# Gate tiles of a hybrid mixer read ahead, two heads' attention steps called later, one warming product fewer

## The chip, the cores and the metric

The kernel runs on one core of one Trainium2 chip, as one launch. The metric is device time in microseconds (us): lower is better. A run is one execution; the median of the runs shown is the time that is compared. One further execution was taken with the hardware profiler; all durations of single instructions come from it.

## The reference, cut to what matters

One block on x of 512 rows by 1024 columns, float32: half a SwiGLU feed-forward step, a mixer, half a SwiGLU step, a norm.

```
x = x + 0.5 * swiglu(rmsnorm(x), ffn1)              # 1024 -> 2 * 2816 -> 1024
h = rmsnorm(x)
cb, cc, cu, q, k, v, g_lr, r, ga, gb = split(h @ w_in)
y_conv = (cb * short_conv(cc * cu)) @ w_out_conv
o      = gla_chunked(q, k, v, log_sigmoid(g_lr @ up + b) / 16)   # 4 heads, chunks of 64
y_gla  = (norm(o) * silu(r)) @ w_out_gla
x = x + (sigmoid(ga) * y_conv + sigmoid(gb) * y_gla) @ w_o
x = x + 0.5 * swiglu(rmsnorm(x), ffn2)
return rmsnorm(x)
```

ga and gb are 512 x 1024 each. The kernel holds each as eight tiles of 128 x 512 (four blocks of rows t, two halves of columns e).

## The kernel before

**Products.** Every operand v is split into a high part h (a cast to the short fp32r type, on ACT) and a low part l = v - h (a subtraction, on DVE), and a product is three products: h·h, h·l, l·h. For weights this is `W.issue`: L380 makes wh on ACT, L381 makes wl on DVE. The tiles wh and wl have three buffers each, and W runs two steps ahead of PE. So each step of PE (12 products of 512 columns at L696, or 24 of 256 columns at L613) needs one L380 and one L381 of its own before its second product.

**Strassen-like steps.** Large products go in seven steps (m1, p2, q6, p5, q7, p3, p4) over quarter matrices. The weights' quarters a11, a12, a21, a22 are loaded by SP (L343, 512 KB each) into tiles f. Sums of quarters are made in three ways: by POOL as accumulating DMAs (L347: a21 += a22, then after m1 a11 += a21, then after p2 a12 += a11), by DVE for q7 (L374: a11 -= a22, which must wait until the accumulating DMA of a12 += a11 has read a11), and by DVE at L359 for the sets. A "tall" product (names v, ga, gb, out) runs each step twice, for two halves s = 0 and 1 of the inner dimension; a "set" (numbered 0 to 7) runs it once.

**Order of the work.** The mixer runs: q and k; the talls v, ga, gb; the eight sets (four for the convolution, two for cb, two for r); the tall out (y_conv); w_out_gla in two halves e; w_o. Inside `run_sets` PE's order is the program's, by a manual schedule. DVE, ACT, SP and POOL are ordered by a scheduler, which sees the order of the calls and its own estimate of when operands are ready; `keep_in_program_order` only keeps an instruction behind the one called before it on its engine.

**Hooks.** Between steps, the table `hooks` calls the pieces of the attention of each head: `gates` (decays' logarithms), `decays` (two DVE subtractions, L1336 and L1339), `exps` (five small activations on ACT), `scale`, `scale_k`, `scale_q` (nine DVE multiplications through `mul`, L583), `scores` (PE products L1385, L1387, transposes L1398), `state` (PE L1410, DVE L1414), `output` (PE L1427, L1430), `squares`, `normalise`. A key such as ("gb", 0, "p2") means: after half 0 of step p2 of gb; (3, "m1") means: after step m1 of set 3.

**Gates.** When a tile of ga or gb is complete, ACT stores it to DRAM (L1484). While w_out_gla runs, `gate` (L1684) takes a free working tile tp, reads the tile back on SP's queue (L1686, 256 KB), applies the sigmoid on ACT (L1687) and DVE multiplies: m = y_conv * sigmoid(ga) at L583, then, when a half of w_out_gla is done, the product with sigmoid(gb) (L583) and the sum (L1726). PE needs m only for the transposes L1699 ahead of w_o.

**Start.** Ten products of ones (L277, each two passes on PE) fill PE's time until the first operands are there.

Of the kernel before, what the change touches and what calls it, by code (L numbers as in the profile page):

```python
# [11 lines left out]
AF = mybir.ActivationFunctionType  # L12
# [15 lines left out]
NTB = S // P  # L28
# [6 lines left out]

V_G1, V_GM, V_G2, V_GLA, V_CONV, V_GB = 0, 8, 16, 24, 32, 56
NVEC = 60
WARM = 10
ODD_FILL = 272

TAIL = 4
# [191 lines left out]
def block_kernel(ctx: ExitStack, tc: tile.TileContext, xT, vecs, gf, gup, wgl, wts, out):  # L233
    nc = tc.nc
# [20 lines left out]
    def tile_of(pool, shape, dtype=F32):  # L255
        cnt[0] += 1
        return pools[pool].tile(shape, dtype, tag=pool, name=f"{pool}{cnt[0]}")

    def T(dtype=F32):
        return tile_of("tp", [P, S], dtype)  # L260
# [5 lines left out]
    def AUX():  # L266
        cnt[0] += 1
        return pa.tile([P, S], F32, tag="aux", name=f"aux{cnt[0]}")
# [6 lines left out]
    warm = AUX()  # L275
    for i in range(WARM):
        nc.tensor.matmul(warm[:, :P], ones, ones, start=True, stop=True)  # L277
# [6 lines left out]
    def big(name):  # L284
        return keep.tile([P, KD, S], F32, tag="X", name=name)
# [296 lines left out]
    def mul(out_, a, b, eng=None):  # L582
        (eng or nc.vector).tensor_tensor(out=out_, in0=a, in1=b, op=ALU.mult)  # L583
# [608 lines left out]
    def mixer(norm, nxt):  # L1192
# [3 lines left out]
        gates_d = {n: dram.tile([KD, P, S], F32, tag=n, name=n) for n in ("ga", "gb")}  # L1196
# [7 lines left out]
        def flat(i):  # L1204
            at = 2 * (S + 2) * i
            return YS.rearrange("p e t -> p (e t)")[:, at : at + 1024]

        def two(i):
            return flat(i).rearrange("p (e t) -> p e t", e=2)
# [6 lines left out]
        def G_tile(i, dtype=F32):  # L1216
            cnt[0] += 1
            return pools["g"].tile([P, S], dtype, tag=f"g{i}", name=f"g{i}_{cnt[0]}")

        sc = pools["g"].tile([P, S], F32, tag="sc", name="sc")  # L1220
# [9 lines left out]
            out=maskf, in_=maskf, pattern=[[1, P]], compare_op=ALU.is_ge, fill=0.0,  # L1230
# [76 lines left out]
        def pairs(t):  # L1307
            return t.rearrange("p (b e t) -> p b e t", e=2, t=CH)
# [10 lines left out]
        def gates(h):  # L1319

            a = AUX()
            nc.tensor.matmul(a, gup_w[:R3, h * DK : (h + 1) * DK], glr[:R3],
                             start=True, stop=True)
            b = vec[:, V_GB + h : V_GB + h + 1]
            nc.scalar.activation(E, a, AF.Abs, bias=b)
            nc.vector.tensor_scalar(out=M, in0=a, scalar1=b, scalar2=0.0,
                                    op0=ALU.add, op1=ALU.min)
            nc.scalar.activation(E, E, AF.Exp, scale=-1.0)
            nc.scalar.activation(E, E, AF.Ln, bias=1.0)
            nc.vector.tensor_tensor(out=M, in0=M, in1=E, op=ALU.subtract)  # L1330
            nc.vector.tensor_tensor_scan(out=E, data0=reset, data1=M, initial=0.0,
                                         op0=ALU.mult, op1=ALU.add)
# [18 lines left out]
        def bc(t):  # L1351
            return t.unsqueeze(2).to_broadcast([P, NTB, CH])

        def scale(h):

            q_, k_ = QK[h][:, 0], QK[h][:, 1]
            ref = sm4[:, 0]
            mul(q_, EX, q_)  # L1360
            mul(KX, pairs(KS)[:, :, 0], pairs(k_)[:, :, 0])
            mul(QX, pairs(q_)[:, :, 1], bc(ref[:, :, 1]))

        def scale_k(h):

            k_, dc = QK[h][:, 1], sm4[:, 1]
            mul(pairs(KS)[:, :, 1], pairs(KS)[:, :, 1], pairs(k_)[:, :, 1])
            mul(k_, M, k_)
            mul(pairs(KS)[:, :, 0], KX, bc(dc[:, :, 1]))

        def scale_q(h):

            q_ = QK[h][:, 0]
            ref, dc = sm4[:, 0], sm4[:, 1]
            mul(pairs(QS)[:, :, 1], QX, bc(dc[:, :, 0]))
            mul(pairs(QS)[:, :, 0], pairs(q_)[:, :, 0], bc(ref[:, :, 0]))
            mul(d2s, dc[:, :, 0], dc[:, :, 1])

        def scores(h):

            q_, k_ = QK[h][:, 0], QK[h][:, 1]
            st = AUX()
            for t in range(NTB):
                b = slice(t * P, (t + 1) * P)
                nc.tensor.matmul(st[:, b], k_[:, b], q_[:, b], start=True, stop=True)  # L1385
            for t in range(NTB):
                nc.tensor.matmul(st[:CH, t * P + CH : (t + 1) * P], KX[:, t], QX[:, t],  # L1387
                                 start=True, stop=True)
            nc.vector.copy_predicated(
                sc.rearrange("p (b i) -> p b i", i=P),  # L1390
                mask.unsqueeze(1).to_broadcast([P, NTB, P]),
                st.rearrange("p (b i) -> p b i", i=P),
            )
            n = NTB - 1
            tr = AUX()
            for t in range(n):
                b = slice(t * P, (t + 1) * P)
                nc.tensor.transpose(tr[:, b], KS[:, b], ident)  # L1398
            nc.scalar.copy(E[:, : n * P], tr[:, : n * P])

        def state(h):

            v = vt[h // 2]
            kvs = []
            for t in range(NTB - 1):
                if t % 2 == 0:
                    kv = AUX()
                hc = slice((t % 2) * DV, (t % 2) * DV + DV)
                kvs.append(kv[:, hc])
                nc.tensor.matmul(kvs[t], E[:, t * P : (t + 1) * P],  # L1410
                                 v[t][:, (h % 2) * DV : (h % 2) * DV + DV], start=True, stop=True)
            nc.scalar.copy(ST[0], kvs[0])
            for t in range(1, NTB - 1):
                nc.vector.scalar_tensor_tensor(out=ST[t], in0=ST[t - 1], scalar=d2s[:, t : t + 1],  # L1414
                                               in1=kvs[t], op0=ALU.mult, op1=ALU.add)
# [114 lines left out]
        def split_o(h):  # L1530
            for a, b in split_pair(O[h]):
                og_h.append(a)
                og_l.append(b)

        hooks = {
            ("v", 0, "q6"): [decays, exps], ("v", 1, "p5"): [lambda: scale(0)],
            ("v", 0, "q7"): [lambda: scale_k(0)],
# [1 line left out]
            ("ga", 1, "m1"): [lambda: state(0)], ("ga", 1, "p2"): [lambda: output(0)],  # L1539
            ("ga", 0, "p5"): [lambda: squares(0)], ("ga", 1, "p5"): [lambda: gates(1)],  # L1540
            ("ga", 0, "q7"): [decays], ("ga", 1, "q7"): [exps],
            ("ga", 0, "p3"): [lambda: scale(1)], ("ga", 1, "p3"): [lambda: scale_k(1)],
            ("gb", 0, "m1"): [lambda: scores(1)], ("gb", 1, "m1"): [lambda: scale_q(1)], ("gb", 0, "p2"): [lambda: state(1)],
            ("gb", 1, "q6"): [lambda: output(1)], ("gb", 1, "q7"): [lambda: squares(1)],
            ("gb", 0, "p3"): [move], ("gb", 1, "p3"): [lambda: gates(2)],
            ("gb", 0, "p4"): [decays], (0, "p2"): [exps], (0, "q6"): [lambda: scale(2)],
            (0, "p5"): [lambda: scale_k(2)], (0, "q7"): [lambda: scale_q(2)],
            (0, "p3"): [lambda: scores(2)], (1, "q6"): [lambda: state(2)],
            (1, "q7"): [lambda: output(2)], (1, "p4"): [lambda: squares(2)],
            (1, "p3"): [lambda: gates(3)], (2, "p5"): [decays], (2, "q7"): [exps],  # L1550
            (3, "m1"): [lambda: scale(3)], (2, "p4"): [lambda: scale_k(3)],
            (2, "p3"): [lambda: scale_q(3)],
            (3, "q6"): [lambda: scores(3)], (3, "p3"): [lambda: state(3)],
            (4, "q6"): [lambda: output(3)], (4, "p3"): [lambda: squares(3)],
            (5, "q7"): [lambda: normalise(0)], (5, "p3"): [lambda: normalise(1)],
            (6, "q7"): [lambda: normalise(2)], (6, "p3"): [lambda: normalise(3)],
            ("out", 1, "p5"): [lambda: co.make("p4")], ("out", 0, "q7"): [lambda: split_o(0)],
            ("out", 1, "q7"): [lambda: split_o(1)], ("out", 0, "p3"): [lambda: split_o(2)],
            ("out", 1, "p3"): [lambda: split_o(3)],
        }  # L1560
# [116 lines left out]
        m = [[QK[2 + t // 2][:, t % 2] for t in range(NTB)], vt[1]]  # L1677
        co = Operands(lambda j, l: YS[:, 4 * j : 4 * j + 4, 2 + l * HW : 2 + (l + 1) * HW])
# [3 lines left out]
        finish_late()  # L1682

        def gate(name, t, e):  # L1684
            g = T()
            tc.keep_in_program_order(nc.sync.dma_start(g, gates_d[name][2 * t + e]))  # L1686
            nc.scalar.activation(g, g, AF.Sigmoid)  # L1687
            return g

        m_h, m_l = [], []  # L1690
# [16 lines left out]
        def between(e):  # L1707
            def extra(k):
                if e == 1 and k == 3:
                    XS.append(big("X2"))  # L1710
                    x[:] = [XS[-1][:, k] for k in range(KD)]
                    for k_ in range(KD):
                        nc.gpsimd.dma_start(x[k_], xs[k_])
                if k in (1, 3, 4, 6):
                    t = (1, 3, 4, 6).index(k)
                    mul(m[e][t], m[e][t], gate("ga", t, e))
                if e == 1 and k in (5, 6):
                    turned(2 * (k - 5))
            return extra

        for e in range(2):
            o = mm_wide("w_out_gla", KD, 512 * e, og_h, og_l, extra=between(e))
            for t in range(NTB):
                g = gate("gb", t, e)
                mul(g, o[t], g)
                nc.vector.tensor_tensor(out=m[e][t], in0=m[e][t], in1=g, op=ALU.add)  # L1726

# [83 lines left out]
```

## Time and profile before

| | us |
|---|---|
| median of 3 runs | 1168.81 (1168.37 to 1169.87) |
| the profiled execution's own time | 1169.12 |
| its span, first to last instruction | 1167.4 |
| PE busy | 1158.9 |
| DVE busy | 895.1 |
| ACT busy | 657.3 |
| granted TensorE clock | 0.999 of full speed |

The profiled execution's time is 1.7 us over its span, and 0.3 us over the median. In the page's rows a group of instructions is named by line, engine and operation and by its tiles, out<-in. Rows of the timeline give the start (us from the span's start), the duration, the engine, the line and the tiles; a count such as x2 merges instructions that follow each other, and a bracket tells how long the engine was idle before and what ended that. Products of PE overlap: two that follow each other without a wait start 0.227 us (512 columns) or 0.12 us (256 columns) apart, though each is shown as longer.

### The profile page before, as it was taken

How to read it: one execution, taken by the hardware profiler on the slowest of the kernel's cores; microseconds unless marked ns; L12 is line 12 of the kernel's file. 1: busy time of each engine (PE TensorE's matmuls, PEld its weight loads, DVE VectorE, ACT ScalarE, POOL GpSimd, SP SyncE). 2: the span in 40 equal slices, each digit the busy share in tenths (PEclk: the TensorE clock that was granted, in tenths of full speed). 3: DMA queues.
4: the chain of work that ended last, by engine and by line, in shares of the span. 5: the costliest groups of instructions: out<-in, count | busy, mean ns of one | idle time of the engine just before them, and what ended most of it. 6: DMA issues, size and time to landing. Idle time of an engine off the chain costs nothing.

```text
span 1167.4 us, 16527 instructions
## 1 busy us (share of the span) xinstructions
PE 1158.9 (99%) x6428; PEld 1010.3 (87%) x6428; DVE 895.1 (77%) x1066; ACT 657.3 (56%) x832; POOL 127.4 (11%) x167
## 2 busy tenths in 40 slices
PE   9999999999999999999999999999999999999997
PEld 7888888989988888889999998888888888888886
DVE  7985666889887976777797999555876666799966
ACT  6565555634452756475654577525655556575543
POOL 0101110001120110110110112000101101101100
PEclk9999999999999999999999999999999999999999
DMA  9667786657665485878576787834567966877711
GB/s 363 129 183 165 170 219 162 173 131 175 170 207 153 96 223 152 209 208 215 134 174 155 181 205 213 288 109 131 118 181 163 231 171 157 203 176 165 184 48 72
DMA packets 59870, 203.22 MB, mean 174 GB/s; under 512 B 6960, under 2 KB 7088, under 8 KB 59792
## 3 DMA queue, kind: packets, MB, share of 16 engines
q0 software_dynamic: 20288, 73.41, 33.3%
q1 hardware_dynamic: 36912, 124.27, 32.4%
q10 hardware_dynamic: 2592, 4.49, 1.0%
q8 instruction: 50, 0.82, 0.3%
q14 instruction: 28, 0.23, 0.1%
HBM read 124.55 MB, written 8.39 MB: 114 GB/s over the span
## 4 chain that ended last, share of the span: by engine, by line
PE 95%; DVE 2%; ACT 1%; DMA 1%; issue 0%; SPq 0%; ACTq 0%; DVEq 0%
PE mm L696 48%; PE mm L613 23%; PE mm L432 5%; PE mm L408 3%; PE mm L410 3%; PE mm L409 3%; PE aux L840 1%; PE mm L451 1%; PE mm L450 1%; PE mm L449 1%; PE mm L1083 1%; PE mm L1082 1%; PE mm L1081 1%; PE aux L1427 1%; DVE wl L381 1%
## 5 line engine op out<-in xcount | busy, mean ns | idle before, releaser
L380 ACT CAST wh<-f 128x1024 fp32r<-128x1024 f32 (+1 forms) x349 | 365.5, 1049 | 361.3 <-PE mm L696 138.0
L381 DVE TENSOR_TENSOR wl<-f,wh 128x1024 fp32r<-128x1024 f32 (+1 forms) x349 | 424.1, 1217 | 181.2 <-ACT wh L380 180.4
L696 PE MATMUL mm<-wh,op 128*128 128x512 f32 x1680 | 528.1, 391 | 0.0
L696 PEld LDWEIGHTS mm<-wh,op 128*128 128x128 f32 x1680 | 315.5, 188 | 65.8 <-ACT tp L814 0.8
L696 PE MATMUL mm<-wl,op 128*128 128x512 f32 x840 | 327.3, 390 | 0.2 <-DVE wl L381 0.2
L613 PE MATMUL mm<-op,wh 128*128 128x256 f32 x1456 | 263.7, 284 | 0.2 <-ACT tp L618 0.2
L613 PEld LDWEIGHTS mm<-op,wh 128*128 128x128 f32 x1456 | 227.0, 191 | 1.1 <-ACT tp L618 0.4
L347 POOL DMA_DIRECT2D f<-f x132 | 113.8, 865 | 910.5 <-DVE wl L381 434.1
L613 PE MATMUL mm<-op,wl 128*128 128x256 f32 x728 | 206.1, 283 | 0.3 <-DVE wl L381 0.3
L696 PEld LDWEIGHTS mm<-wl,op 128*128 128x128 f32 x840 | 157.8, 188 | 32.6 <-DVE wl L381 1.0
L613 PEld LDWEIGHTS mm<-op,wl 128*128 128x128 f32 x728 | 139.1, 191 | 0.5 <-DVE wl L381 0.5
L668 ACT CAST op<-hid 128x1024 fp32r<-128x1024 f32 x42 | 44.0, 1050 | 23.2 <-PE mm L696 11.0
L669 DVE TENSOR_TENSOR op<-hid,op 128x1024 fp32r<-128x1024 f32 x42 | 51.1, 1217 | 2.9 <-ACT op L668 2.9
L408 PE MATMUL mm<-op,wh 128*128 128x512 f32 x132 | 51.4, 389 | 0.0
L409 PE MATMUL mm<-op,wh 128*128 128x512 f32 x132 | 51.4, 389 | 0.0
L410 PE MATMUL mm<-op,wl 128*128 128x512 f32 x132 | 51.4, 389 | 0.0
L432 PE MATMUL mm<-op,wh 128*128 128x512 f32 x192 | 48.3, 393 | 0.3 <-ACT wh L380 0.2
L374 DVE TENSOR_TENSOR f<-f,f 128x1024 f32<-128x1024 f32 x30 | 36.6, 1220 | 10.9 <-DMA f<-f 8.6
L432 PEld LDWEIGHTS mm<-op,wh 128*128 128x128 f32 x192 | 35.6, 188 | 8.8 <-ACT wh L380 1.1
L408 PEld LDWEIGHTS mm<-op,wh 128*128 128x128 f32 x132 | 24.8, 188 | 5.2
L409 PEld LDWEIGHTS mm<-op,wh 128*128 128x128 f32 x132 | 24.8, 188 | 5.2
L410 PEld LDWEIGHTS mm<-op,wl 128*128 128x128 f32 x132 | 24.8, 188 | 5.1
(326 smaller groups left out, 1194.8 us busy)
## 6 DMA issues: line engine op xcount, KB each, us to landing
f<-wts SPq DMA_DIRECT2D x219, 512.0 KB, 4.3
f<-f POOLq DMA_DIRECT2D x132, 512.0 KB, 5.1
X<-xT SPq DMA_DIRECT2D x8, 256.0 KB, 5.7
xs<-X POOLq DMA_DIRECT2D x8, 256.0 KB, 2.8
ga<-tp ACTq DMA_DIRECT2D x8, 256.0 KB, 5.2
gb<-tp ACTq DMA_DIRECT2D x8, 256.0 KB, 3.9
tp<-ga SPq DMA_DIRECT2D x8, 256.0 KB, 5.1
X<-xs POOLq DMA_DIRECT2D x8, 256.0 KB, 7.3
```

What stands on the lines that cost most here:

```text
L347: nc.gpsimd.dma_start(out_, a, accum_op=ALU.add)
L374: nc.vector.tensor_tensor(out=a11, in0=a11, in1=a22, op=ALU.subtract)
L380: nc.scalar.copy(h[:, :w], raw[:, :w])
L381: nc.vector.tensor_tensor(out=l[:, :w], in0=raw[:, :w], in1=h[:, :w].bitcast(F32), op=ALU.subtract)
L408: nc.tensor.matmul(o, wh, ah, start=first, stop=False)
L409: nc.tensor.matmul(o, wh, al, start=False, stop=False)
L410: nc.tensor.matmul(o, wl, ah, start=False, stop=last)
L432: nc.tensor.matmul(o[c], w[:, s : s + P], a[k], start=k == 0 and j == 0, stop=k == kt - 1 and j == 2)
L613: nc.tensor.matmul(to, ww[:, s], aa[:, t], start=fresh and k == 0 and e == 0 and j == 0, stop=k == 3 and j == 2, skip_group_check=True)
L668: nc.scalar.copy(hv, v)
L669: nc.vector.tensor_tensor(out=lv, in0=v, in1=hv.bitcast(F32), op=ALU.subtract)
L696: nc.tensor.matmul(self.bank[b][e], aa[:, c], ww, start=fresh and i == 0 and n == 0, stop=k == 3 and n == 2, skip_group_check=True)
```

## The change

It does four things.

1. **All sixteen gate tiles are read ahead, into tiles that are free by then.** The four tiles (ga, e = 0) go into three tiles of the attention (G_tile 2, 3 and 4) and `sc`; the hook `fetch_gates` after ("out", 0, "m1") issues their reads. The four (gb, e = 0) go into the lower half of the convolution's tile YS, called after ("out", 0, "q7"); the four (ga, e = 1) into its upper half, after ("out", 0, "p4"); the four (gb, e = 1) into the first four tiles again, at k = 0 of the second half of w_out_gla. Working tiles tp are no longer taken for gates.
2. **Sigmoids stand at fixed places**: of (ga, e = 0) in hooks of the tall out, the others at k = 1, 3, 4, 6 of the two halves of w_out_gla. Their number is the same, sixteen, and so are the reads.
3. **Steps of heads 1 and 3 are called later.** Head 1: scale, scale_k, scores, scale_q and state, by one or two half steps. Head 3: decays, exps, scale and scale_k, by one step.
4. **WARM is 9, not 10.**

```
-WARM = 10
+WARM = 9
...
+        ahead = {}
+
+        def fetch_gates():
+            for t, g in enumerate((G_tile(2), G_tile(3), G_tile(4), sc)):
+                tc.keep_in_program_order(nc.sync.dma_start(g, gates_d["ga"][2 * t]))
+                ahead[t] = g
+
+        def open_gate(t):
+            tc.keep_in_program_order(nc.scalar.activation(ahead[t], ahead[t], AF.Sigmoid))
+
+        def fetch_more(name, e):
+            for t in range(NTB):
+                g = two(2 * e + t // 2)[:, t % 2]
+                tc.keep_in_program_order(nc.sync.dma_start(g, gates_d[name][2 * t + e]))
+                ahead[name, t, e] = g
...
-            ("ga", 0, "p3"): [lambda: scale(1)], ("ga", 1, "p3"): [lambda: scale_k(1)],
-            ("gb", 0, "m1"): [lambda: scores(1)], ("gb", 1, "m1"): [lambda: scale_q(1)], ("gb", 0, "p2"): [lambda: state(1)],
+            ("ga", 1, "p3"): [lambda: scale(1)], ("ga", 1, "p4"): [lambda: scale_k(1)],
+            ("gb", 1, "m1"): [lambda: scores(1)], ("gb", 0, "p2"): [lambda: scale_q(1)],
+            ("gb", 1, "p2"): [lambda: state(1)],
...
-            (1, "p3"): [lambda: gates(3)], (2, "p5"): [decays], (2, "q7"): [exps],
-            (3, "m1"): [lambda: scale(3)], (2, "p4"): [lambda: scale_k(3)],
+            (1, "p3"): [lambda: gates(3)], (2, "q7"): [decays], (3, "m1"): [exps],
+            (2, "p4"): [lambda: scale(3)], (3, "p2"): [lambda: scale_k(3)],
...
+            ("out", 0, "m1"): [fetch_gates], ("out", 1, "q6"): [lambda: open_gate(0)],
+            ("out", 0, "p5"): [lambda: open_gate(1)],
+            ("out", 1, "p5"): [lambda: co.make("p4"), lambda: open_gate(2)],
+            ("out", 0, "q7"): [lambda: split_o(0), lambda: fetch_more("gb", 0)],
+            ("out", 0, "p4"): [lambda: fetch_more("ga", 1), lambda: open_gate(3)],
...
-            g = T()
-            tc.keep_in_program_order(nc.sync.dma_start(g, gates_d[name][2 * t + e]))
-            nc.scalar.activation(g, g, AF.Sigmoid)
+            g = ahead[name, t, e]
+            tc.keep_in_program_order(nc.scalar.activation(g, g, AF.Sigmoid))
...
+                if e == 1 and k == 0:
+                    for t in range(NTB):
+                        ahead["gb", t, 1] = ahead[t]
+                        tc.keep_in_program_order(
+                            nc.sync.dma_start(ahead[t], gates_d["gb"][2 * t + 1]))
...
-                    mul(m[e][t], m[e][t], gate("ga", t, e))
+                    mul(m[e][t], m[e][t], ahead[t] if e == 0 else gate("ga", t, e))
+                    gate("gb", t, e)
...
-                g = gate("gb", t, e)
+                g = ahead["gb", t, e]
```

**Where instructions move.** First DVE's queue around head 1's scaling, in the steps p3 and p4 of the tall ga (L381 is a step's wl, L583 with y or g the scaling of head 1, L1469 a sum of the tall ga). Before:

```order
L583 TENSOR_TENSOR g_538_3455<-g_538_3455,y_3223 128x4x64
L583 TENSOR_TENSOR g_539_3456<-g_538_3455,y_3223 128x256
L583 TENSOR_TENSOR g_539_3456<-y_3223,sm 128x256
L381 TENSOR_TENSOR wl_4221<-f_3851,wh_4220 128x1024
L1469 SCALAR_TENSOR_TENSOR tp_4082<-mm_4086,tp_4082 128x512
L1469 SCALAR_TENSOR_TENSOR tp_4084<-mm_4087,tp_4084 128x512
L583 TENSOR_TENSOR y_3223<-g_537_3454,y_3223 128x512
L583 TENSOR_TENSOR g_538_3455<-g_539_3456,sm 128x4x64
L381 TENSOR_TENSOR wl_4244<-f_4143,wh_4243 128x1024
```

The same place now:

```order
L583 TENSOR_TENSOR g_538_3454<-g_538_3454,y_3222 128x4x64
L381 TENSOR_TENSOR wl_4217<-f_3850,wh_4216 128x1024
L1469 SCALAR_TENSOR_TENSOR tp_4081<-mm_4085,tp_4081 128x512
L1469 SCALAR_TENSOR_TENSOR tp_4083<-mm_4086,tp_4083 128x512
L583 TENSOR_TENSOR g_539_3455<-g_538_3454,y_3222 128x256
L583 TENSOR_TENSOR g_539_3455<-y_3222,sm 128x256
L381 TENSOR_TENSOR wl_4240<-f_4142,wh_4239 128x1024
L583 TENSOR_TENSOR y_3222<-g_537_3453,y_3222 128x512
```

Two small multiplications moved behind the first L381 and the two L1469, and a full and a small one behind the second L381. Further on, in gb, the two L1414 of head 1's state moved behind the two L1469 and a L381, and on PE the scores and the state of head 1 stand 12 products later.

Second, DVE's queue around head 3's decays (L1579 and L1581 are the convolution; after the change these two lines are L1600 and L1602). Before:

```order
L1581 SCALAR_TENSOR_TENSOR y_3223<-y_3223,vec,tp_5304 128x512
L1581 SCALAR_TENSOR_TENSOR y_3223<-y_3223,vec,tp_5308 128x512
L1336 TENSOR_TENSOR g_537_3454<-g_536_3453 128x512
L1339 TENSOR_TENSOR g_538_3455<-g_536_3453 128x512
L381 TENSOR_TENSOR wl_5323<-f_4786,wh_5322 128x1024
```

Now:

```order
L1602 SCALAR_TENSOR_TENSOR y_3222<-y_3222,vec,tp_5303 128x512
L1602 SCALAR_TENSOR_TENSOR y_3222<-y_3222,vec,tp_5307 128x512
L381 TENSOR_TENSOR wl_5320<-f_4785,wh_5319 128x1024
L1336 TENSOR_TENSOR g_537_3453<-g_536_3452 128x512
L1339 TENSOR_TENSOR g_538_3454<-g_536_3452 128x512
```

The step's wl moved ahead of both subtractions.

Third, DVE's queue in the tall out, around q7's weights (L374 with its two halves, the L381 of p5's two halves, L1674, now L1695, a split of the attention's result). Before:

```order
L374 TENSOR_TENSOR f_6452<-f_6452,f_6458 128x1024
L381 TENSOR_TENSOR wl_6756<-f_6456,wh_6755 128x1024
L374 TENSOR_TENSOR f_6521<-f_6521,f_6527 128x1024
L381 TENSOR_TENSOR wl_6772<-f_6525,wh_6771 128x1024
L669 TENSOR_TENSOR op_6838<-y_3223,op_6837 128x1024
L1674 TENSOR_TENSOR op_6860<-O,op_6859 128x1024
L381 TENSOR_TENSOR wl_6798<-f_6452,wh_6797 128x1024
```

Now:

```order
L374 TENSOR_TENSOR f_6451<-f_6451,f_6457 128x1024
L374 TENSOR_TENSOR f_6520<-f_6520,f_6526 128x1024
L381 TENSOR_TENSOR wl_6762<-f_6455,wh_6761 128x1024
L381 TENSOR_TENSOR wl_6778<-f_6524,wh_6777 128x1024
L669 TENSOR_TENSOR op_6846<-y_3222,op_6845 128x1024
L1695 TENSOR_TENSOR op_6869<-O,op_6868 128x1024
L583 TENSOR_TENSOR qk_3223<-qk_3223,g_995_6688 128x512
L381 TENSOR_TENSOR wl_6805<-f_6451,wh_6804 128x1024
```

Both L374 now stand ahead of the L381 of p5's first half, and a gate's multiplication stands ahead of the L381 of q7's first half. On ACT the table load and one sigmoid stand ahead of the L380 of p5's first half, and on SP the four reads of (ga, e = 0) stand ahead of the last two weight loads that were issued before 700 us, and the four of (gb, e = 0) right behind those. POOL's order is unchanged.

More of the change, by code (lines that the diff above doesn't have):

```diff
@@ L1556, in mixer @@
             (6, "q7"): [lambda: normalise(2)], (6, "p3"): [lambda: normalise(3)],
-            ("out", 1, "p5"): [lambda: co.make("p4")], ("out", 0, "q7"): [lambda: split_o(0)],
+            ("out", 0, "m1"): [fetch_gates], ("out", 1, "q6"): [lambda: open_gate(0)],
[3 more added lines that the diff above has]
+            ("out", 0, "p4"): [lambda: fetch_more("ga", 1), lambda: open_gate(3)],
             ("out", 1, "q7"): [lambda: split_o(1)], ("out", 0, "p3"): [lambda: split_o(2)],
```

## Prediction

> **What bounds the kernel now.** I read the page's table of engines first, then PE's waits, then the timeline wherever PE waited and wherever the change moves something. The page's row of busy times and, from the waits of PE, the rows of weights' low parts:
>
> ```profile
> span 1167.4 us, 16527 instructions
> PE 1158.9 (99%) x6428; PEld 1010.3 (87%) x6428; DVE 895.1 (77%) x1066; ACT 657.3 (56%) x832; POOL 127.4 (11%) x167
> ```
>
> ```profile
> PE mm L613 <- DVE wl L381: 0.3, 1, 0.3
> PE mm L696 <- DVE wl L381: 0.2, 1, 0.2
> ```
>
> PE is the bound: it works through 1158.9 of 1167.4 us. The products themselves stay, so whatever the change brings must come out of places where PE stood still. The waits name only two late wl in the region of the change, and they understate them, since a modelled end of a product reaches into the pause. So I measure the loss at both by the distance between starts, in the timeline.
>
> Head 1, in the last steps of the tall ga. The rows are DVE's queue (L583 scales, L1469 sums, L381 makes wl) and PE's products:
>
> ```profile
> 470.04 0.75 DVE L583 TENSOR_TENSOR g<-g,y 128x256 f32<-128x256 f32 x2
> ...
> 471.05 1.21 DVE L381 TENSOR_TENSOR wl<-f,wh 128x1024 fp32r<-128x1024 f32 x1
> 472.19 1.27 DVE L1469 SCALAR_TENSOR_TENSOR tp<-mm,tp 128x512 f32<-128x512 f32 x2
> 473.38 0.67 DVE L583 TENSOR_TENSOR y<-g,y 128x512 f32<-128x512 f32 x1
> 473.98 0.41 DVE L583 TENSOR_TENSOR g<-g,sm 128x256 f32<-128x256 f32 x1
> ...
> 474.32 1.21 DVE L381 TENSOR_TENSOR wl<-f,wh 128x1024 fp32r<-128x1024 f32 x1
> 474.73 0.61 PE L696 MATMUL mm<-wh,op 128*128 128x512 f32 x2
> 475.58 0.50 PE L696 MATMUL mm<-wl,op 128*128 128x512 f32 x1 [0.23 <-DVE wl L381]
> 475.92 0.62 PE L696 MATMUL mm<-wh,op 128*128 128x512 f32 x2
> ```
>
> Three products at 0.227 us make 0.68; from 474.73 to 475.92 there are 1.19. **0.51 us** are lost, and the L381 begun at 474.32, which ends at 475.53, is the cause.
>
> Head 3, in set 2 (L1336 is the first of the decays' two subtractions):
>
> ```profile
> 582.26 1.98 ACT L380 CAST wh<-f 128x1024 fp32r<-128x1024 f32 x2
> ...
> 583.73 0.68 DVE L1336 TENSOR_TENSOR g<-g 128x512 f32<-128x512 f32 x1
> ...
> 584.93 1.21 DVE L381 TENSOR_TENSOR wl<-f,wh 128x1024 fp32r<-128x1024 f32 x1
> ...
> 585.49 0.40 PE L613 MATMUL mm<-op,wh 128*128 128x256 f32 x2
> 586.20 0.39 PE L613 MATMUL mm<-op,wl 128*128 128x256 f32 x1 [0.32 <-DVE wl L381]
> 586.42 0.40 PE L613 MATMUL mm<-op,wh 128*128 128x256 f32 x2
> ```
>
> Three products at 0.12 make 0.36; from 585.49 to 586.42 there are 0.93. **0.57 us** are lost.
>
> **The change part by part.**
>
> *Gate tiles read ahead.* From the waits of ACT between 700 and 790 us (total, times, longest), and from the busy times by stage (length, then PE, PEld, DVE, ACT and POOL busy, granted clock, DMA share, GB/s):
>
> ```profile
> ACT tp L1687 <- DMA tp<-ga: 11.9, 6, 3.6
> ```
>
> ```profile
> 697.00:712.00 15.00, 15.00 (x70) 12.44 (x69) 15.00 (x16) 10.79 (x12) 2.58 (x3) 1.00 0.80 172
> ...
> 735.00:781.00 46.00, 46.00 (x213) 38.21 (x212) 23.01 (x29) 19.61 (x29) 0.00 (x0) 1.00 0.57 197
> ```
>
> ACT's sigmoids wait 11.9 us for six reads of ga alone, but PE is busy for 46.00 of the 46.00 us in which this happens. Nobody on the path waits for a gate there, so hiding the reads better is worth 0. What the early reads cost is another matter, the tall out, where DMA is at 0.80 already (below and in the rivals).
>
> *Head 1 later.* After the change the first L381 stands behind only one of the pair begun at 470.04, so it starts at about 470.38 (half of 0.75 later). Successive starts give the rest: 1.14 for L381, 1.2 for the two L1469 (472.19 to 473.38), and two small L583 at 0.34 each (473.98 to 474.32). That is 470.38 + 1.14 + 1.19 + 0.68 = 473.39 for the second L381, whose wl is there at 474.60. PE asks for it two products behind 474.73, at 475.19. Margin 0.59: the whole stall goes, **−0.51**. The full multiplication formerly at 473.38 goes behind this L381, where the next wl is not yet short.
>
> Later the state of head 1 moves behind a wl. The rows are the sum L374 in gb that stands ahead of it, L1414's duration in ns, and PE's first user of its result:
>
> ```profile
> 489.46 1.23 DVE L374 TENSOR_TENSOR f<-f,f 128x1024 f32<-128x1024 f32 x1 [3.45 <-DMA f<-f]
> ...
> 496.49 0.39 PE L1430 MATMUL aux<-g,stt 128*128 128x128 f32 x2
> ```
>
> ```profile
> L1414 DVE SCALAR_TENSOR_TENSOR stt<-g,d,aux x1: 475/475/475, 493.4 to 493.4; 128x256 f32<-128x256 f32 x1
> ```
>
> From 489.46 the new queue holds L374, L381, two L1469, L374, one L1414, L381, then the second L1414: 4 × 1.14 + 1.19 + 2 × 0.475 = 6.70, so stt is there at 496.2. PE wants it at 496.49 less the 0.51 gained, 495.98. This is a wait of 0.2 if the accumulating DMA that released L374 lands when it did, and 0 if it moves up with the products that precede it. I take 0 and keep 0.25 as the bound, since this DMA waits for a wl that itself comes earlier now.
>
> *Head 3 later.* The L381 takes L1336's place at 583.73 and ends at 584.94. Should its wh be the second of the two casts begun at 582.26, done at 584.24, it ends at 585.45. PE asks two products behind 585.49, at 585.61 + 0.12 = 585.73. Either way it is there: **−0.57**, and 0 is the other end if the moved decays or exps hit another step. They are two subtractions of 0.6 each on DVE, now behind the wl, and five small activations on ACT one step later.
>
> *Nine warming products.* The start:
>
> ```profile
> 1.11 4.03 PE L277 MATMUL aux<-ones 128*128 128x128 f32 x20 [1.11 <-POOL ones L274]
> ...
> 4.42 0.49 DVE L481 TENSOR_SCALAR op<-X,vec 128x512 fp32r<-128x512 f32 x1 [4.42 <-DMA X<-xT]
> ...
> 5.06 2.09 PE L432 MATMUL mm<-op,wh 128*128 128x512 f32 x8
> ...
> 7.51 0.60 ACT L380 CAST wh<-f 128x512 fp32r<-128x512 f32 x1
> ...
> 8.16 2.11 PE L432 MATMUL mm<-op,wh 128*128 128x512 f32 x8
> ```
>
> Two of twenty passes are 0.4 us, so the ones end near 4.74. The first true product can't start ahead of its operand, at 4.91; it moves up by at most 0.15. The next eight products start at 8.16 because the L380 of 7.51 ends at 8.11, and that hangs on loads, not on PE. So the 0.15 is lost again there: value 0, bounds −0.15 and, if the granted clock opens later, the rival below.
>
> The Trainium skill, "TensorE: Matmul & The Clock Gate", "What's actually happening", says that the array runs at half clock until it has been busy for a window of about 3.4 us, which runs free of the kernel's start. By this rule the estimate for eighteen passes, 18 × 0.20 = 3.6 us, is still above the window, and the sum would stay.
>
> *The tall out.* DVE and ACT around the first half of p5, PE's request, and L1687's two kinds in ns:
>
> ```profile
> 708.35 1.05 ACT L380 CAST wh<-f 128x1024 fp32r<-128x1024 f32 x1 [0.76 <-ACT op L668]
> ...
> 709.21 1.21 DVE L374 TENSOR_TENSOR f<-f,f 128x1024 f32<-128x1024 f32 x1
> ...
> 710.35 1.21 DVE L381 TENSOR_TENSOR wl<-f,wh 128x1024 fp32r<-128x1024 f32 x1
> ...
> 711.48 1.21 DVE L374 TENSOR_TENSOR f<-f,f 128x1024 f32<-128x1024 f32 x1
> ...
> 713.77 0.39 PE L696 MATMUL mm<-wl,op 128*128 128x512 f32 x1
> ```
>
> ```profile
> L1687 ACT ACTIVATE tp<-tp x16: 621/632/637, 724.3 to 762.3; 128x512 f32<-128x512 f32 x16
> L1687 ACT ACT_TABLE_LOAD  x1: 1283/1283/1283, 723.0 to 723.0; - x1
> ```
>
> Both L374 now come first. L381 of p5's first half starts at 711.48, not 710.35, and ends at 712.69, 1.08 ahead of PE's request. Its wh gets the table load and a sigmoid ahead of it on ACT: 708.35 + 1.28 + 0.63 + 1.05 = 711.31, just ahead of 711.48. A gate's multiplication (0.6 to 0.7) ahead of q7's L381 eats into the margin of a step that PE reaches 5.4 us later; nothing is late. Cost 0, as long as the second L374 isn't kept waiting. It waits for the last accumulating DMA of L347. That group between 685 and 712 us, and then only the landing times of the same line between 470 and 487 us, where ACT's stores run beside it:
>
> ```profile
> L347 POOL DMA_DIRECT2D f<-f x6: 860/860/860, 685.1 to 704.4; - x6
> ...
> DMA to landing us min/median/max: 4.5/5.1/5.8
> ```
>
> ```profile
> DMA to landing us min/median/max: 4.5/7.0/8.6
> ```
>
> Issued at 704.4, it lands by 710.2 at the slowest of its group. L374 + L381 need 1.13 + 1.21, so it must land by 713.77 − 2.34 = 711.43. SP's new reads, 1 MB for (ga, e = 0) and 1 MB for (gb, e = 0) behind the last weights, fall into the stretch in which it flies. I take 5.8 us (these neighbours are the same place); 8.6 us, ending at 713.0, is kept for the range.
>
> The Trainium skill, "DMA: Bandwidth & Descriptors", "Queues, rings and completion order", says that each DMA engine takes turns, a packet at a time, between the queues that have work. The trace agrees: a median of 5.1 us here and of 7.0 beside ACT's stores. By this rule the early reads speak against the change, since the accumulation would slow down; it is the first rival.
>
> The sum: −0.51 − 0.57 + 0 + 0 + 0 = −1.08. The profiled execution's own 1169.12 becomes 1168.04; the median of 1168.81 lies 0.31 below it and becomes **1167.7**.
>
> **The rivals.**
>
> *The reads hold up the accumulating DMA in the tall out (slower).* At 0.80 share and 172 GB/s the engines would move 215 GB/s when full; 1 MB then takes 4.9 us. If all of it goes ahead, the DMA lands at 710.2 + 4.9 = 715.1, and PE waits 3.7 us; by 8.6 us it lands at 713.0, and PE waits 1.6. Net +0.5 to +2.6: 1169.3 to 1171.4. It decides from a landing at 711.43. For it: DMA's share, and the new order of L374 ahead of L381. Against: the DMA needs 1.2 us more than its slowest neighbour to do harm.
>
> *The clock opens later.* If the nine products no longer open the granted clock, the eight products that begin at 5.06 run at half rate: 8 × 0.227 = 1.8 us more, of which the pause ahead of 8.16 takes back about 0.2. Net +0.5: 1169.3. Against it: in the trace the products behind 5.06 are at full pace already, eight in 2.09, after 4.03 us of ones. By the free-running window of the Trainium skill's page on TensorE (the section named above), eighteen passes could fall short of a full window.
>
> *Half of it.* One stall stays or reappears at the neighbouring step, or stt is late by its 0.25: 1168.0 to 1168.4.
>
> *More of it.* The earlier steps also save a few tenths at the start and where the shorter queues let later wl be early: 1166.9 to 1167.4.
>
> *No effect at all.* If the stalls only move to the next wl, 1168.8; for it speaks that DVE is full (15.00 of 15.00) in part of the out.
>
> **How the numbers follow.** Forecast 0.63, half of it 0.16, more of it 0.08, accumulation late 0.06, clock 0.04, no effect 0.03. The three runs shown lie 1.5 us apart, so a median carries some half a us of its own. The range from 1166.6 to 1169.2 holds the forecast, the halves, the more and no effect; it leaves out most of the first two rivals. A measurement of this kernel can tell about 0.2%, 2.34 us, from no change. Faster than 1166.47 needs twice the forecast: 0.05. Slower than 1171.15 needs the accumulation late by nearly all of its 4.9 us: 0.04. The same: 0.91.
>
> **What would show it right or wrong.** Right: no bracket with wl L381 on PE's rows near 475 and 586, triples at 0.68 and 0.36 there, L1430's first row unmoved but for the gain, and a span about 1.1 us shorter. The start: the product formerly at 8.16 within 0.1 of it. Out: L374's second row at about 709.2 to 710.4 less 1.1, with no idle time that ends on a DMA. Wrong: a row of PE near 713 that waits for L381, or L374 waiting for f; PE rows of L432 at 0.45 spacing; or a span that is shorter by over 2.3 us, which would mean that PE lost time in the gates' stretch that the starts do not show.

## The result and the profile after

The changed kernel takes 1173.53 us (median of 6 runs, 1172.77 to 1174.65), the kernel before 1169.33 beside it: a ratio of 1.0037, 95% interval 1.0026 to 1.0048. It is **slower by 4.2 us**; forecast was 1.1 us faster. Of all the executions below one, of the kernel without both batches, ran at a granted clock of 0.655 and took 1648.62 us; the ratios leave it out. First the page's span and busy times:

```profile
span 1171.9 us, 16515 instructions
...
PE 1160.0 (99%) x6426; PEld 1011.1 (86%) x6426; DVE 895.4 (76%) x1066; ACT 658.1 (56%) x832; POOL 127.4 (11%) x167
```

The span is 4.5 us longer, and PE is hardly busier. Then the waits of PE:

```profile
PE mm L696 <- DVE wl L381: 3.7, 1, 3.7
...
PE mm L613 <- ACT tp L618: 0.4, 1, 0.4
```

There is one large new wait, and both old wl waits are gone. (The 0.4 us behind L618 do not come from the reads: the kernel below that has none in the tall out loses 0.5 there.) The new one stands in the tall out. Its timeline, with POOL's last two accumulating DMAs (L347), SP's reads of the second batch (L1548), DVE and PE:

```profile
703.86 0.86 POOL L347 DMA_DIRECT2D f<-f  x1 [1.94 <-issue]
...
704.89 2.93 SPq L1548 DMA_DIRECT2D y<-gb  x4
...
706.30 0.86 POOL L347 DMA_DIRECT2D f<-f  x1 [1.57 <-DVE wl L381]
...
709.42 1.22 DVE L374 TENSOR_TENSOR f<-f,f 128x1024 f32<-128x1024 f32 x1
...
712.22 0.61 PE L696 MATMUL mm<-wh,op 128*128 128x512 f32 x2
...
714.10 1.22 DVE L374 TENSOR_TENSOR f<-f,f 128x1024 f32<-128x1024 f32 x1 [3.46 <-DMA f<-f]
...
715.25 2.35 DVE L381 TENSOR_TENSOR wl<-f,wh 128x1024 fp32r<-128x1024 f32 x2
...
716.52 0.50 PE L696 MATMUL mm<-wl,op 128*128 128x512 f32 x1 [3.68 <-DVE wl L381]
```

Read it from the end. PE's product at 716.52 waits for the L381 at 715.25; that stands on DVE behind the second L374, which waits until 714.10 for the DMA issued at 706.30. From PE's start at 712.45 (the second of the pair at 712.22) to 716.52 there are 4.07 us, 0.23 of them regular: a pause of 3.84.

The pause costs more than itself. The rows of busy times by stretch (length, PE, PEld, DVE, ACT, POOL, granted clock, DMA share, GB/s):

```profile
712.00:717.00 5.00, 1.32 (x6) 0.81 (x5) 2.90 (x3) 3.98 (x6) 0.00 (x0) 1.00 0.43 124
717.00:722.00 5.00, 5.00 (x17) 3.95 (x16) 5.00 (x6) 1.50 (x2) 0.00 (x0) 0.66 0.81 278
```

Behind the pause the granted clock is 0.66, and PE has 17 products at work in 5 us, where five us at 0.227 hold 22. PE's own rows show when it fell:

```profile
717.32 0.40 PE L696 MATMUL mm<-wl,op 128*128 128x512 f32 x1
717.55 0.77 PE L696 MATMUL mm<-wh,op 128*128 128x512 f32 x2
718.12 0.63 PE L696 MATMUL mm<-wl,op 128*128 128x512 f32 x1
718.55 1.06 PE L696 MATMUL mm<-wh,op 128*128 128x512 f32 x2
```

The first products go at full pace; from 718.12 they start 0.43 apart (718.12 to 718.55), until 721.1. Over the regular 0.227 that comes to 1.7 us. So 3.84 + 1.7 − 1.08 (the two old stalls) = 4.5, the whole difference of the spans.

The accumulating DMAs (L347, between 683 and 712 us) as a group:

```profile
L347 POOL DMA_DIRECT2D f<-f x6: 860/862/862, 684.0 to 706.3; - x6
...
DMA to landing us min/median/max: 4.6/6.6/9.4
```

Before, these were 4.5/5.1/5.8 and the last was issued at 704.4. With the earlier 1.08 us it should have gone out at 703.3: it goes out 3.0 us late and then flies 7.7 us (from issue to landing), to 714.0, instead of 4.8.

The two heads' places turned out as forecast. Head 1 (DVE's L381, then PE's rows at the old stall):

```profile
473.26 1.21 DVE L381 TENSOR_TENSOR wl<-f,wh 128x1024 fp32r<-128x1024 f32 x1
...
474.58 0.61 PE L696 MATMUL mm<-wh,op 128*128 128x512 f32 x2
...
475.04 0.39 PE L696 MATMUL mm<-wl,op 128*128 128x512 f32 x1
475.26 0.61 PE L696 MATMUL mm<-wh,op 128*128 128x512 f32 x2
```

From 474.58 to 475.26 is 0.68: no stall. Head 3:

```profile
583.05 1.22 DVE L381 TENSOR_TENSOR wl<-f,wh 128x1024 fp32r<-128x1024 f32 x1
...
584.18 0.69 DVE L1336 TENSOR_TENSOR g<-g 128x512 f32<-128x512 f32 x1
...
584.81 0.40 PE L613 MATMUL mm<-op,wh 128*128 128x256 f32 x2
585.05 0.28 PE L613 MATMUL mm<-op,wl 128*128 128x256 f32 x1
585.17 0.40 PE L613 MATMUL mm<-op,wh 128*128 128x256 f32 x2
```

584.81 to 585.17 is 0.36. The start, too:

```profile
5.02 2.08 PE L432 MATMUL mm<-op,wh 128*128 128x512 f32 x8
...
8.10 2.11 PE L432 MATMUL mm<-op,wh 128*128 128x512 f32 x8
```

The second set of products, which waits for its L380, starts 0.06 earlier than before.

### The profile page after: what moved, and what is told of

Its sections match the earlier page's. It is cut to its first block, busy times and chain, and to the rows that moved or that the text cites. A ratio compares the mean times of both kernels' runs of the same rounds, so it can differ in the third digit from the quotient of the medians.

```text
span 1171.9 us, 16515 instructions
## 1 busy us (share of the span) xinstructions
PE 1160.0 (99%) x6426; PEld 1011.1 (86%) x6426; DVE 895.4 (76%) x1066; ACT 658.1 (56%) x832; POOL 127.4 (11%) x167
## 4 chain that ended last, share of the span: by engine, by line
PE 95%; DVE 2%; DMA 1%; ACT 1%; issue 0%; SPq 0%; DVEq 0%; ACTq 0%
PE mm L696 48%; PE mm L613 23%; PE mm L432 5%; PE mm L408 3%; PE mm L410 3%; PE mm L409 3%; PE aux L840 1%; PE mm L451 1%; PE mm L449 1%; PE mm L450 1%; DMA f<-f 1%; DVE wl L381 1%; PE mm L1083 1%; PE mm L1081 1%; PE mm L1082 1%; PE aux L1427 1%
## 5 line engine op out<-in xcount | busy, mean ns | idle before, releaser
L380 ACT CAST wh<-f 128x1024 fp32r<-128x1024 f32 (+1 forms) x349 | 365.4, 1049 | 383.6 <-PE mm L696 133.3
L381 DVE TENSOR_TENSOR wl<-f,wh 128x1024 fp32r<-128x1024 f32 (+1 forms) x349 | 424.2, 1217 | 189.9 <-ACT wh L380 187.9
L696 PE MATMUL mm<-wh,op 128*128 128x512 f32 x1680 | 529.5, 392 | 0.0
L696 PEld LDWEIGHTS mm<-wh,op 128*128 128x128 f32 x1680 | 316.2, 188 | 66.1 <-ACT tp L814 0.8
L696 PE MATMUL mm<-wl,op 128*128 128x512 f32 x840 | 328.0, 391 | 3.7 <-DVE wl L381 3.7
L347 POOL DMA_DIRECT2D f<-f x132 | 113.9, 863 | 906.6 <-DVE wl L381 366.4
L696 PEld LDWEIGHTS mm<-wl,op 128*128 128x128 f32 x840 | 158.2, 188 | 36.3 <-DVE wl L381 4.7
L374 DVE TENSOR_TENSOR f<-f,f 128x1024 f32<-128x1024 f32 x30 | 36.6, 1221 | 10.9 <-DMA f<-f 9.8
```

The costliest lines, as they stand in the source:

```text
L347: nc.gpsimd.dma_start(out_, a, accum_op=ALU.add)
L374: nc.vector.tensor_tensor(out=a11, in0=a11, in1=a22, op=ALU.subtract)
L380: nc.scalar.copy(h[:, :w], raw[:, :w])
L381: nc.vector.tensor_tensor(out=l[:, :w], in0=raw[:, :w], in1=h[:, :w].bitcast(F32), op=ALU.subtract)
L696: nc.tensor.matmul(self.bank[b][e], aa[:, c], ww, start=fresh and i == 0 and n == 0, stop=k == 3 and n == 2, skip_group_check=True)
```

## The experiments

The theory after the result (A): both early batches of reads are needed for the loss. The first, (ga, e = 0) at 687.5 to 689.5, delays POOL's accumulating DMAs, so that the last of them is issued late; the second, (gb, e = 0) from 704.9, slows the flight of that one. The margin of 1.2 us is overrun, and the long pause then costs PE its clock. Rivals: one batch alone does it (B the second, C the first); the new order of DVE or the sigmoids cost by themselves; the heads' part isn't the gain it seems.

**The heads' part alone**, gates as before:

```diff
-WARM = 10
+WARM = 9
...
-("ga", 0, "p3"): [lambda: scale(1)], ("ga", 1, "p3"): [lambda: scale_k(1)],
+("ga", 1, "p3"): [lambda: scale(1)], ("ga", 1, "p4"): [lambda: scale_k(1)],
...
-(1, "p3"): [lambda: gates(3)], (2, "p5"): [decays], (2, "q7"): [exps],
+(1, "p3"): [lambda: gates(3)], (2, "q7"): [decays], (3, "m1"): [exps],
...
```

> The kernel before with the two heads' later steps and nine warming products alone; gates as before. Theory: the heads' part brings the forecast 1.08 us (0.51 at head 1, 0.57 at head 3) and the ones nothing, so about 1168.2 against 1169.3, no wait of PE for wl near 475 and 585. Rival: the new places cost something elsewhere, 1169.3 or more.

Measured: 1168.14 us (11 runs) against 1169.52; ratio 0.9989, interval 0.9981 to 0.9998. That is −1.4, and the profile's PE waits name no wl any more. The forecast's own sum holds for this part. It is the one version here with the whole result whose interval lies below before, and it is the change without its gates.

**Without the first batch, without the second, without both.** The sigmoids stay, on a tile that is there already, so each of these three kernels leaves a part of the result out; DVE, PE and POOL keep the order of after, ACT its sigmoids in the same places. The edits (first batch, then second):

```diff
-                tc.keep_in_program_order(nc.sync.dma_start(g, gates_d["ga"][2 * t]))
...
-            tc.keep_in_program_order(nc.scalar.activation(ahead[t], ahead[t], AF.Sigmoid))
+            tc.keep_in_program_order(nc.scalar.activation(ahead[t], O[0][:, 0], AF.Sigmoid))
```

```diff
-                tc.keep_in_program_order(nc.sync.dma_start(g, gates_d[name][2 * t + e]))
+                if name == "ga":
+                    tc.keep_in_program_order(nc.sync.dma_start(g, gates_d[name][2 * t + e]))
...
+            v = O[0][:, 0] if (name, e) == ("gb", 0) else g
-            tc.keep_in_program_order(nc.scalar.activation(g, g, AF.Sigmoid))
+            tc.keep_in_program_order(nc.scalar.activation(g, v, AF.Sigmoid))
```

> After, without the four reads of (ga, e = 0): their sigmoids read a tile that is there already (so this part of the result is left out); all other queues keep their order. Theory A (both batches are needed): the last accumulating DMA is issued at about 703.3 to 704 again and lands by 708 to 711.4, so PE waits 0 to 1.1 us in the tall out and its clock stays up: 1168.2 to 1169.3. Theory B (the second batch alone does it): landing at 714 and 1173.5 stay.

> After, without the four reads of (gb, e = 0), their sigmoids on a tile that is there (this part of the result is left out); all other queues keep their order. Theory A: the accumulating DMA is still issued at 706.3 but lands within 4.8 to 5.1 us, at 711.1 to 711.4; PE waits 0.8 to 1.1 us and keeps its clock: 1169.0 to 1169.4. Theory B (second batch alone): no wait, 1168.2. Theory C (first batch alone): 1173.5.

> After, without both batches of reads (that part of the result is left out); sigmoids, multiplications and the order of DVE, ACT, POOL and PE as in after. Theories A, B and C: the loss is all in the transfers, so 1168.2, landing at 708 to 709. Rival: the new order of DVE or the sigmoids and the table load in the tall out cost by themselves: over 1169.3.

L347 without the first batch, without the second, without both, and in each case L374's rows. A bracket means that the second L374 waited. It names the L374 before it, which had ended 0.5 to 0.7 us earlier; what came last was the DMA, which lands at 709.2 in the first case and at 710.1 in the second, by its own time to landing in the table:

```profile
L347 POOL DMA_DIRECT2D f<-f x6: 860/860/860, 683.4 to 703.1; - x6
...
709.24 1.23 DVE L374 TENSOR_TENSOR f<-f,f 128x1024 f32<-128x1024 f32 x1 [0.51 <-DVE f L374]
```

```profile
L347 POOL DMA_DIRECT2D f<-f x6: 860/860/862, 683.2 to 705.2; - x6
...
710.18 1.23 DVE L374 TENSOR_TENSOR f<-f,f 128x1024 f32<-128x1024 f32 x1 [0.72 <-DVE f L374]
...
712.60 0.50 PE L696 MATMUL mm<-wl,op 128*128 128x512 f32 x1 [0.58 <-DVE wl L381]
```

```profile
L347 POOL DMA_DIRECT2D f<-f x6: 860/860/860, 683.3 to 702.6; - x6
...
707.41 2.35 DVE L374 TENSOR_TENSOR f<-f,f 128x1024 f32<-128x1024 f32 x2
```

| | last DMA issued | its time to landing | second L374 starts | PE's pause | time, ratio to before (interval) |
|---|---|---|---|---|---|
| neither batch | 702.6 | 4.8 | 708.5, no wait | 0 | 1167.97, 0.9990 (0.9979 to 1.0000) |
| second only | 703.1 | 6.1 | 709.2 | 0 | 1168.18, 0.9990 (0.9980 to 0.9999) |
| first only | 705.2 | 4.9 | 710.2 | 0.74 | 1168.52, 0.9994 (0.9985 to 1.0003) |
| both (after) | 706.3 | 7.7 | 714.1 | 3.84 | 1173.53, 1.0037 (1.0026 to 1.0048) |

Theory A holds, B and C fall: each batch alone nearly fits into the margin, the two together overrun it. The pause without the second batch was a little shorter than A said, and its time 0.5 under A's range (1168.52 for 1169.0 to 1169.4). The second batch only lengthens the flight, from 4.8 to 6.1 us; the first only delays the issue, by 2.6 us, with a flight of 4.9. Together they come to more than their sum, and the likely reason is the order: a DMA that is issued late goes out among the four reads (704.89 to 707.82) instead of ahead of them. In every trace here in which it does, it takes 7.1 to 8.7 us. The rival that blames DVE's order or the sigmoids falls with the kernel without both: it has them and loses nothing. One of its runs took 1173.13 us, and two of the kernel with the second batch only took 1170.62 and 1171.47; why is not known.

How the first batch delays the issue is seen in POOL's queue, after and then without both batches:

```profile
694.68 0.86 POOL L347 DMA_DIRECT2D f<-f  x1 [2.71 <-DMA f<-wts]
701.06 0.86 POOL L347 DMA_DIRECT2D f<-f  x1 [5.52 <-DMA f<-f]
```

```profile
693.96 0.86 POOL L347 DMA_DIRECT2D f<-f  x1 [2.67 <-DVE wl L381]
697.35 0.86 POOL L347 DMA_DIRECT2D f<-f  x1 [2.52 <-DMA f<-wts]
```

Without the reads the fourth issue (697.35) waits for a weight load; in after (701.06) it waits for an accumulating DMA, the second of the group, which is the 9.4 us of the group's maximum. Issued at 691.11, it flies beside the reads until 693.6 and then beside the two weight loads that stand behind them on SP's queue, which take 8.1 and 9.3 us themselves, where before no weight load of this stretch took over 5.8. Without both batches the group's maximum is 6.4, without the second alone 9.2. The issues that follow pass the delay on to the last.

**Other order, same reads.** First, with the sigmoids of (ga, e = 0) called in w_out_gla, which gives DVE the order of before; then, with the second L374 held further back:

```diff
-            ("out", 0, "m1"): [fetch_gates], ("out", 1, "q6"): [lambda: open_gate(0)],
-            ("out", 0, "p5"): [lambda: open_gate(1)],
-            ("out", 1, "p5"): [lambda: co.make("p4"), lambda: open_gate(2)],
+            ("out", 0, "p5"): [fetch_gates],
+            ("out", 1, "p5"): [lambda: co.make("p4")],
...
+                    if e == 0:
+                        open_gate(t)
```

> After, with the sigmoids of (ga, e = 0) called at k = 1, 3, 4, 6 of w_out_gla instead of in the tall out; the reads stand in SP's queue where after has them, but DVE has the order of before (the L381 of p5's first half between the two L374). Theory A: landing near 714, the L381 of p5's second half is done at about 716.4 and asked for at 715.4, so a pause of about 1 us and no loss of clock: 1169.1 to 1169.5. Rival (the late landing costs the same in either order): 1173.5. Rival (no collision once the sigmoids are gone): 1168.2.

```diff
-                        nc.vector.tensor_tensor(out=a11, in0=a11, in1=a22, op=ALU.subtract)
+                        sub = nc.vector.tensor_tensor(out=a11, in0=a11, in1=a22, op=ALU.subtract)
+                        if TALL[n][0] == "out":
+                            tc.keep_in_program_order(sub)
```

> After, with DVE's second L374 (the one that waits for the last accumulating DMA) held behind the L381 of both halves of p5 and of q7's first half; all reads stay where after has them. Theory A: the DMA still lands at about 714, but only q7's second half hangs on it, which PE reaches 8 us after p5's first half, so no pause and no loss of clock: 1168.2 against 1169.3 to 1169.5 of before. Rival: the wait moves to q7, or the loss comes from the transfers in another way: over 1170.

The first: 1169.70 us against 1169.47 (ratio 1.0004, 0.9995 to 1.0013). Its second L374, and the PE row that waited:

```profile
714.76 1.23 DVE L374 TENSOR_TENSOR f<-f,f 128x1024 f32<-128x1024 f32 x1 [3.29 <-issue]
...
717.18 0.50 PE L696 MATMUL mm<-wl,op 128*128 128x512 f32 x1 [2.00 <-DVE wl L381]
```

The DMA lands as late as in after (issued at 706.0, 8.7 us to landing; the bracket names no releaser), but p5's first half is already supplied; the second waits, 2.2 us and not the 1 expected, and the clock stays at 1.00 behind it. Another 0.5 us is lost at q7, and the time is 0.2 over the expected range. The second: 1168.91 us against 1169.47 (0.9993, 0.9984 to 1.0002), 0.7 over the expectation and far under the rival's 1170. The rows of its second L374 and of PE (L698 is L696 two lines further down):

```profile
717.68 1.21 DVE L374 TENSOR_TENSOR f<-f,f 128x1024 f32<-128x1024 f32 x1
...
722.36 0.50 PE L698 MATMUL mm<-wl,op 128*128 128x512 f32 x1 [0.31 <-DVE wl L383]
```

The late landing costs nothing directly, since L374 stands where nobody asks for it yet; 0.3 is lost at p5 and 0.6 to 0.9 at q7's second half, whose wl now stands behind other work. So the transfers make the DMA late, and DVE's order decides whether PE pays.

**PE kept busy in the pause**, by products of ones ahead of p5's first half; in the second try with L1695 held behind the L381 of q7's second half:

```diff
+                if (name, half, p) == ("out", 0, "p5"):
+                    filler = AUX()
+                    for _ in range(12):
+                        nc.tensor.matmul(filler[:, :P], ones, ones, start=True, stop=True)
```

and, in the second try alone:

```diff
-            nc.vector.tensor_tensor(out=l, in0=v, in1=h.bitcast(F32), op=ALU.subtract)
+            r = nc.vector.tensor_tensor(out=l, in0=v, in1=h.bitcast(F32), op=ALU.subtract)
+            if len(og_h) == 2:
+                tc.keep_in_program_order(r)
```

> After, with twelve products of ones (24 passes, about 2.6 us) ahead of p5's first half in the tall out, inside the pause. Theory A (PE's clock falls because it stands still for 3.8 us): the pause that is left is about 1.2 us, the products behind it start 0.227 apart, the 1.9 us of slow products go: 1171.4 to 1171.8. Rival (the slow products have another cause, as DMA traffic or weights): 1173.5; if the filler only delays, 1175 or more.

> The filler again, twelve products of ones in the pause, now with the second split of the attention's result (L1695) held behind the L381 of q7's second half, so that DVE's queue gives no new wait near 725. Theory: the pause keeps its end, the clock stays up behind it, and the eight products at 0.43 us are gone, so 1.6 to 1.9 us under the run of after beside it (about 1171.7, mean clock 0.999 against 0.997). Rival: the clock's dip costs nothing that the span shows, and the time is that of after within 0.5.

> The changed kernel once more, unaltered, on the chip of the filler run, as the reference for it: 1173.5, a pause of 3.5 to 4 us in the tall out and some eight products at 0.43 us behind it, if both belong to the kernel and not to one execution.

The first try took 1174.11 us (5 runs), 2.3 over A's range. Its profile is the plain test of the clock: the second L374 starts at 714.44, as late as in after, PE's longest idle stretch there is 1.4 us, and behind it the granted clock is 1.00. But DVE's queue had changed, and PE lost 0.8 at 726 (the second row below) and 1.2 more in ffn2 behind L818; the latter isn't explained.

```profile
717.00:722.00 5.00, 5.00 (x22) 4.09 (x23) 5.00 (x6) 2.36 (x4) 0.00 (x0) 1.00 0.80 250
...
726.01 0.50 PE L696 MATMUL mm<-wl,op 128*128 128x512 f32 x1 [0.65 <-DVE wl L381]
```

The second try took 1172.35 (11 runs), the unaltered kernel on the same chip 1174.31 (5 runs): −2.0, though their ratios to before, 1.0024 (1.0015 to 1.0033) and 1.0035 (1.0021 to 1.0049), overlap in their intervals. The unaltered kernel paused as expected, for 3.94 us, but some thirteen products behind it, not eight, went at 0.43. Its pause, and the stretches behind the pause, with the filler and then without:

```profile
711.89 0.61 PE L696 MATMUL mm<-wh,op 128*128 128x512 f32 x2
716.28 0.79 PE L696 MATMUL mm<-wl,op 128*128 128x512 f32 x1 [3.78 <-DVE wl L381]
```

```profile
717.00:722.00 5.00, 5.00 (x24) 4.13 (x23) 4.88 (x6) 2.83 (x4) 0.00 (x0) 1.00 0.97 357
```

```profile
716.30:722.00 5.70, 5.70 (x14) 4.44 (x15) 5.67 (x6) 0.62 (x1) 0.00 (x0) 0.50 0.81 271
```

Over the whole run the mean clock was 0.998 to 1.000 in all eleven runs with the filler, and 0.996 to 0.998 in four of five without; the fifth had 0.999 and took 1170.98. In the filler's profiled execution the DMA landed earlier (L374 at 712.6; without the filler the pause would, by an estimate from these starts, have been some 2.4 us), so this profile says nothing on the clock, and how much of the 2.0 us is the clock and how much an earlier landing stays open. That PE's standing still is what drops the clock rests on the first try's profile: the same late landing, traffic beside it, and no fall once PE is kept busy.

**The gates alone**, heads and warming products as before:

```diff
-WARM = 9
+WARM = 10
...
-("ga", 1, "p3"): [lambda: scale(1)], ("ga", 1, "p4"): [lambda: scale_k(1)],
+("ga", 0, "p3"): [lambda: scale(1)], ("ga", 1, "p3"): [lambda: scale_k(1)],
...
```

> The gates' part of the change alone, heads and warming products as before. Theory: the two parts add up. After is 4.2 slower than before, the heads' part gave 1.2 to 1.4, so 5.4 to 5.6 slower than before: 1174.7 to 1175.1. Rival: the earlier heads drew the accumulating DMAs into the reads, so that the gates alone cost less, 1172 or under.

Measured: 1173.35 us (4 runs, 1170.90 to 1176.03) against 1169.47, +3.9; ratio 1.0040, 1.0024 to 1.0056. The measured value lies between the two expectations; the interval reaches from 2.8 to 6.5 us, holds the theory's 5.4 to 5.6 and ends close above the rival's 2.5. With four runs that scatter by 5 us it is undecided whether the parts add up. The profiled run is the shortest; in it PE paused for 2.5 us and kept its clock:

```profile
715.37 0.50 PE L696 MATMUL mm<-wl,op 128*128 128x512 f32 x1 [2.37 <-DVE wl L381]
```

## Why the prediction was wrong

- **What bounds it, and the two stalls: right.** Both went, at the places and by the amounts named; alone, with the nine warming products, they give −1.4 measured for −1.08 forecast, within the interval (−2.2 to −0.2).
- **Gates read ahead are worth nothing to PE: right.** Without any reads in the tall out the kernel is no faster than with the heads' part alone (1167.97 and 1168.14).
- **Head 1's state, and nine warming products: no cost found**, as taken. The waits of PE show neither; the start is 0.06 us earlier.
- **The tall out at cost 0: the step that failed.** It said "Issued at 704.4, it lands by 710.2 at the slowest of its group" and took 5.8 us because "these neighbours are the same place". Two things in it were wrong. The issue was held fixed, though the first batch slows an earlier accumulating DMA, for which POOL's later ones wait: 2.6 us. And the flight was taken from neighbours that had no gate reads beside them, when the change puts reads there: 7.7 us.
- **The first rival had the mechanism and its threshold right.** It decided from a landing at 711.43, which is 710.35 on the shifted clock; the DMA landed at 714.0, 3.7 late, and PE paused 3.84. Its upper price of 3.7 was nearly met, but by another sum: it put 4.9 us of transfer, from engines that it took to move 215 GB/s when full, on a DMA issued in time. What was measured is an issue 3.0 late and a flight 2.9 longer than the 4.8 of before, and in after the engines moved 307 GB/s between 690 and 697 us, so agreement in size is luck. What the rival lacked was the issue's delay as a cause, and the 1.7 us of reduced clock behind the pause, which no step of the prediction spoke of. Its chance of 0.06 rested on asking whether the reads would be slow enough, not on adding up both batches' effects along POOL's queue.
- **The rule of the Trainium skill on DMA queues taking turns** ("DMA: Bandwidth & Descriptors", "Queues, rings and completion order") spoke against the change and was given too little weight; the runs agree with it in direction, 4.8 to 4.9 us without the second batch and 6.1 to 7.7 with it.
- **The clock rival at the start** did not decide, though the half pace it feared occurred: where the first four true products went at half pace (0.43 us, in the heads' run), the pause ahead of the second set was gone and the ninth product began at 7.77, the second set at 8.69, and the third at 11.40 as against 11.38 before.

## What to carry to other kernels

A transfer that is read early for a consumer that nobody waits for is not free: follow it into every queue that it passes or runs beside, to the next instruction with a small margin. If two effects on one chain each eat most of the same margin, add them along the chain before giving either a chance. And where a wait on a DMA stands ahead of another instruction's supply on one engine, moving that wait back can win most of what a faster transfer would: 1168.91 us here with the DMA as late as ever, against 1167.97 without the reads and 1173.53 with the wait in front.

## What the runs showed of the hardware

- PE's granted clock can fall around the end of a pause. Pauses of 2.2 and 2.5 us left it at 1.00. Of 3.84 us (after) it fell to half pace some 1.5 us after PE had resumed, for 3 us; in the second execution of the same kernel (3.94 us) it was at half pace as soon as PE resumed, for some 5.7 us. The cost is 1.7 and 2.8 us on top of the pause. The Trainium skill's "TensorE: Matmul & The Clock Gate" ("What's actually happening") gives an idle window of about 3.4 us; the pauses here lie on both sides of it and agree, but none lies between 2.5 and 3.84 us, so they do not test the figure closely.
- Nine warming products gave full pace at once in one execution (eight products in 2.08 us) and half pace for four products in another (2.96 us), in two programs that start alike (after, and the heads' part alone).
